# Attention results with features on the partitions (values stationary, two heads at once) and a feature-major second gate, in a two-block transformer kernel

## The chip, the core and the metric

The kernel runs on one core of a Trainium2 chip. A core has five engines, each with its own queue of instructions in fixed order: TensorE (PE; matmuls and transposes), VectorE (DVE), ScalarE (ACT), GpSimd (POOL) and SyncE (SP), which mostly issues transfers. Engines wait for each other on semaphores. The metric is the device time of one execution in microseconds (us); less is better.

## The reference

Two transformer blocks run one after the other on 256 tokens of width 1024, in float32.

```python
# first block, cut
fox_out  = softmax(q k^T/8 + forget bias, causal) @ v              # 8 heads of 64
diff_out = (softmax(q1 k1^T + alibi) - lam*softmax(q2 k2^T + alibi)) @ v   # 4 heads, v of 128
diff_out = _rms(diff_out, diff_norm_g[l]) * (1.0 - lam_init)
mixed = concatenate([fox_out, diff_out], axis=-1)
x = x + g1 * (mixed @ w_out[l])
h2 = _modulate(x, ln2_g[l], sh2, sc2)
x = x + g2 * ((silu(h2 @ w_gate[l]) * (h2 @ w_up[l])) @ w_down[l])
# second block, cut
za_u, za_v, q, k, v_att, g_a, g_b = split(rms_norm(x) @ w_in)
y_a = sgu_mixer(gelu(za_u), gelu(za_v), ...)
y_b = moba_attention(q, k, v_att, rel_bias)                        # 16 heads of 64
merged = sigmoid(g_a) * y_a + sigmoid(g_b) * y_b
x = x + merged @ w_out
x = x + square(relu(rms_norm(x) @ w_ff1)) @ w_ff2
x = x + sigmoid(rms_norm(x) @ w_ple_gate) * (p @ w_ple_proj)
return rms_norm(x)
```

## The kernel before

**Tiles.** The 256 tokens are two tiles t of 128 tokens on the partitions. A float32 matrix is split in a high and a low part: for a weight, ScalarE writes `wh` (a rounded copy of `raw`, which a transfer brought) and VectorE `wl` (raw minus wh). A product is then three matmuls, high by high, high by low and low by high (`mm3`); such three are called a triple here. A matmul of plain float32 operands (PV, the statistics `ap` and `pb`) is one instruction in the program and two records in the trace. Attention results and norm inputs are split in the same way (`mTh`, `mTl`).

**Attention.** `attention()` (L726 to L773) serves the fox attention (name `fa`) and the two halves of the moba attention (`ma0`, `ma1`), each of 8 heads. For a tile t and a pair of head groups it makes `scores` (s), `softmax` (VectorE adds the bias and takes the maximum, ScalarE exponentiates, which leaves unnormalised probabilities and their sums), four transposes (`tr4`, pt), a copy on ScalarE (pT), and PV: pT is the stationary operand (128 columns), the values of one head (64 columns) are moving, and the result (`pv`) has tokens on the partitions. When all groups of t are done, VectorE multiplies `pv` by the reciprocal sums into `mixed` or `yb`. Names read as attention, t, first head of the pair, member: fa120 is tile 1, pair 2, member 0. `diff_group` (L966 to L1023, name `da`) does this for the difference attention with its own normalisation (the two probabilities are scaled and subtracted before the transposes), its PV (`dpv`), and at the end a root mean square over each head: square (dsq) on ScalarE, sum (dss) on VectorE, an inverse root (dn) on GpSimd, multiplication into `mixed`, four transposes (mt) and the split into `mTh`, `mTl`. `fox_out` (L1035 to L1044) transposes the fox half of `mixed` (mf) and splits it.

**Out-projection.** `out_proj` (L1171 to L1185) takes the halves h of the features (0 fox, 1 diff), in each the tiles t, in each two column blocks of 512: four triples each, so 24 matmuls for a half and a tile. `wo` is the first block's, `wo2` the second's. Behind it come the residual (rg, x on VectorE), the second norm (n2j, n2x on ScalarE, n2a, n2r on GpSimd, transposes n2t) and `up`, the first product of the feed-forward part.

**Second block.** `ga` and `gb` are the two gates; `gate` (L1641) takes each in tiles of tokens (weights moving, 512 columns), and `merge` (L1658 to L1671) adds the two branches, transposes the sum (mt2) and splits it for `wo2`.

**What sets the order.** The instructions of all engines are written out by generators that a planner steps: it keeps a clock for each engine from its own table of costs and runs a generator on when what it waits for should be there. `slot` asks for room in the accumulators, `flag` for another generator's mark, `on` and `onp` for data. `room` (L723) opens a new attention group only while `groups[0]` is under a limit, which is 3 in this part; a fox pair adds 2 at its start and each member takes 1 off behind its PV; a diff group adds and takes 1. One piece of work is kept as filler for TensorE: the products `ppa` of the last stage (p @ w_ple_proj), given away in pieces where the planner sees TensorE idle, once the out-projection's mark is set (`spare`, L1295). What comes out is one fixed queue for each engine.

Of the kernel before, what the change touches and what calls it, by code (L numbers as in the profile page):

```python
# [10 lines left out]
F32 = mybir.dt.float32  # L11
# [6 lines left out]
P = 128  # L18
# [188 lines left out]
def body(ctx, tc, ins, out):  # L207
# [144 lines left out]
    def on(*aps, slack=None):  # L352
        return lambda: pace.when(*aps) <= clock["PE"] + (par(SLACK) if slack is None else slack)
# [275 lines left out]
    use(("dk", 1), True)  # L629


    def piece(acc, x_, k, u, first, last, a=0):

        for j in range(4):
            wh, wl = use(k, h=j // 2)
            kt = u * 4 + j
# [86 lines left out]
    def room():  # L723
        return groups[0] < par(ROOM)

    def attention(qT, kT, bias, extra, row, vt, vflag, dst, name):  # L726

        state = {}

        def pair(t, n, heads):  # L730
            yield slot(2), room, calm
            groups[0] += 2
            nm = f"{name}{t}{n}"
            for q, sp in enumerate(scores(qT, kT, heads, t, extra, nm)):
                run(group(t, sp, heads[q], f"{nm}{q}"))

        def group(t, sp, heads, nm):
            yield on(sp[:, :len(heads) * (t + 1) * P])
            pe, sm = yield from softmax(sp, heads, t, bias, None if row is None else row(t), nm)
            yield onp(pe), slot()  # L740
            rs = state[t]["rs"]
            V.reciprocal(rs.rearrange("p (a b) -> p b a", b=2)[:, heads[0] % 2, heads[0] // 2:heads[0] // 2 + len(heads)],
                         sm[:, :len(heads)])
# [24 lines left out]
        def launch():  # L768
            for t in range(NT):
                state[t] = {"rs": small(f"{name}{t}rs", 8), "n": len(HG[t])}  # L770
# [31 lines left out]
    mixed = [slab(f"mixed{t}") for t in range(NT)]  # L802

    def log_forget(z, e, lf):

# [141 lines left out]
    def fox_start():  # L947
        yield flag("fox_qk", "fox_c")
        attention(fqkT[0], fqkT[1], lambda h, nk: al[:, 4, 256 - nk:256], (selr, R), fox_row,
                             lambda k: vv[k][:, 0:512], "fv1", [m[:, 0:512] for m in mixed], "fa")  # L950


    def keep(dst, kflag, scale=None):
# [12 lines left out]
    def diff_group(t, n, h0, gs):  # L966
# [39 lines left out]
        if dstate[t]["n"]:  # L1006
# [8 lines left out]
        V.tensor_tensor(mixed[t][:, 512:1024].rearrange("p (h d) -> p h d", d=P), pv.rearrange("p (h d) -> p h d", d=P),  # L1015
                        r.unsqueeze(2).broadcast_to([P, 4, P]), op=ALU.mult)
        free(pv)
        yield onp(mixed[t][:, 512:1024]), slot(), lambda: len(mT) > t
        pt = tr4(mixed[t][:, 512:1024], 4, f"mt{t}")
        yield on(pt)  # L1020
        split_act(pt, 4, mT[t][0], mT[t][1], 4, pfs("dng"))
        free(pt)
        flags.add(f"mT1{t}")  # L1023

# [5 lines left out]
            for n, h0 in enumerate(range(0, 4, gs)):  # L1030
                run(diff_group(t, n, h0, gs))

    mT = []

    def fox_out():  # L1035
        for t in range(NT):
            yield flag("fa0", "fa1"), onp(mixed[t][:, 0:512]), slot()
            mT.append((slab(f"mTh{t}", F32R).rearrange("p (k t) -> p k t", t=P),
                       slab(f"mTl{t}", F32R).rearrange("p (k t) -> p k t", t=P)))
            pt = tr4(mixed[t][:, 0:512], 4, f"mf{t}")  # L1040
            yield on(pt)
            split_act(pt, 4, mT[t][0], mT[t][1], 0)
            free(pt)
            flags.add(f"mT0{t}")  # L1044

    rows2, bz, ap2 = {}, {}, {}
# [83 lines left out]
    run(lam(), 2)  # L1132
    run(diff_qk())
    run(diff())
    run(fox_out())
# [35 lines left out]
    def out_proj(name, mTs, mflag, fin):  # L1171
        acc = {}
        for h in range(2):
            for t in range(NT):
                until(flag(f"{mflag}{h}{t}"))
                until(on(mTs[t][0][:, h * 4:h * 4 + 4, :], mTs[t][1][:, h * 4:h * 4 + 4, :]))
                for cb in range(2):
                    if h == 0:
                        acc[t, cb] = psA(f"{name}{t}{cb}")
                    piece(acc[t, cb], mTs[t], (name, h, cb), h, h == 0, h == 1)  # L1180
# [117 lines left out]
    run(ple_prep())  # L1298
    run(ple_proj(), 2)
    hT_n, *hT_all = hT_tiles("n2")  # L1300
    out_proj("wo1", mT, "mT", residual(0, norm_shift("n2", hT_n, "n2")))
    hT = hT_n


    def feature_piece(acc, k, f):


        for kt in range(KT):
            wh, wl = use(k + (kt // 4,), h=kt % 4 // 2)
            c = slice((kt % 4) * 512 + f * P, (kt % 4) * 512 + f * P + P)  # L1310
            T.matmul(acc, lhsT=wh[:, c], rhs=hT_all[2][:, kt, :], start=kt == 0, stop=False)
            T.matmul(acc[:, 0:256], lhsT=wl[:, c], rhs=hT_all[0][:, kt, :], start=False, stop=kt == KT - 1)
            if kt % 2 and kt < KT - 1:
                tick()

# [215 lines left out]
            return self.d[self.k + (t,)] if self.k else self.d[t]  # L1531

    rs3 = Late(rstd, "n3")
    yb = [slab(f"yb{t}") for t in range(NT)]
    vm = [slab(f"vm{t}") for t in range(NT)]

    rrow = half("rrow")
# [36 lines left out]
    for hf in range(2):  # L1574
        qk = [slab(f"{nm}T{hf}").rearrange("p (a t) -> p a t", t=256) for nm in ("q", "k")]
        proj(("v", hf), keep(lambda t: vm[t][:, hf * 512:(hf + 1) * 512], f"mv{hf}", rs3), None if hf else "n3")
        proj_T(("q", hf), qk[0], 0, f"mq{hf}")
        proj_T(("k", hf), qk[1], 1, f"mk{hf}")

        def moba(hf=hf, qk=qk):  # L1580
            yield flag(*(f"m{c}{hf}{f}" for c in "qk" for f in range(4))), on(qk[0], qk[1])
            attention(qk[0], qk[1], lambda h, nk: rev(hbs[0][:, hf * 8 + h, 0:nk]), None, None,
                                 lambda k: vm[k][:, hf * 512:(hf + 1) * 512], f"mv{hf}1",
                                 [y[:, hf * 512:(hf + 1) * 512] for y in yb], f"ma{hf}")
        run(moba())


# [65 lines left out]

    for hf in range(2):
        proj(("ga", hf), gate(ya, hf, "ya"))
    mT2 = []

    def merge(t, hf):  # L1658
        yield flag(f"gya{hf}{t}")
        c = slice(hf * 512, hf * 512 + 512)  # L1660
        V.tensor_tensor(yb[t][:, c], yb[t][:, c], ya[t][:, c], op=ALU.add)
        if not mT2:
            for q in range(NT):
                mT2.append((slab(f"m2h{q}", F32R).rearrange("p (k t) -> p k t", t=P),
                            slab(f"m2l{q}", F32R).rearrange("p (k t) -> p k t", t=P)))
        yield onp(yb[t][:, c]), slot()
        pt = tr4(yb[t][:, c], 4, "mt2")
        yield on(pt)
        split_act(pt, 4, mT2[t][0], mT2[t][1], 4 * hf)
        free(pt)  # L1670
        flags.add(f"mU{hf}{t}")  # L1671

    for hf in range(2):
        proj(("gb", hf), gate(yb, hf, f"ma{hf}", merge))
    st["phase"] = 3
    until(lambda: len(mT2) == 2)
    out_proj("wo2", mT2, "mU", residual(None, norm_plain("n4", Lazy("n4"), pcs("nffn"), "n4", after4)))
    hT = lazy("n4")
    hT_all = late["n4"][1:]
    st["phase"] = 4  # L1680
# [220 lines left out]
```

## Time and profile before

| | |
|---|---|
| runs (us) | 786.88, 786.51, 786.5; median 786.51 |
| profiled execution | 787.08 us, its span 785.3 us |
| TensorE busy | 770.6 us (98%) |
| VectorE, ScalarE busy | 520.4 us (66%), 424.9 us (54%) |
| GpSimd busy | 34.4 us |
| the chain that ended last | PE 91%, ACT 3%, DVE 3%, issue 1%, DMA 1% |

The sum of an edit is made against the profiled execution, whose rows give the durations: 0.57 us above the median. All helpers record the line L153, so groups are told apart by the names of their tiles, written out<-in.

### The profile page before, as it was taken

To read this page: it belongs to the slowest core of one execution; us is meant where nothing else is said; L and a number is where in the kernel's file an instruction comes from. 1 tells how busy PE (TensorE), PEld (TensorE's weight loads), DVE (VectorE), ACT (ScalarE), POOL (GpSimd) and SP (SyncE) were. 2 spreads that over 40 slices of the span, in tenths; PEclk is the share of its full clock that TensorE was granted. 3 is DMA by queue.
4 is the path that set the end of the run, shared out by engine and by line. 5 is a ranking of instruction groups with operands and counts; after the bars stand their busy time and mean duration, and the time that the engine had idled before them with its cause. 6 is when DMAs were issued, how large, how long until landed. Compare 5 with 4: busy or idle time off the path is not lost.

```text
span 785.3 us, 10687 instructions
## 1 busy us (share of the span) xinstructions
PE 770.6 (98%) x4110; PEld 631.6 (80%) x4110; DVE 520.4 (66%) x913; ACT 424.9 (54%) x711; POOL 34.4 (4%) x73
## 2 busy tenths in 40 slices
PE   8999999999999999999999999999999999999996
PEld 7777667778888888888879878888888888888885
DVE  4878867667576866558674658746676665566583
ACT  4457467466554554456556584554475455445463
POOL 0000000121100000001100001000010000000011
PEclk9999999999999999999999999999999999999999
DMA  8967853755855666534762334545555544554331
GB/s 338 413 245 300 291 192 126 285 220 193 321 214 215 240 230 227 199 124 159 297 214 68 148 108 161 215 167 209 187 174 203 190 162 184 214 214 183 138 108 54
DMA packets 25251, 159.61 MB, mean 203 GB/s; under 512 B 2944, under 2 KB 3104, under 8 KB 8816
## 3 DMA queue, kind: packets, MB, share of 16 engines
q1 hardware_dynamic: 23184, 152.27, 52.0%
q0 software_dynamic: 2016, 6.66, 2.5%
q8 instruction: 32, 0.52, 0.3%
q14 instruction: 19, 0.16, 0.1%
HBM read 156.80 MB, written 2.12 MB: 202 GB/s over the span
## 4 chain that ended last, share of the span: by engine, by line
PE 91%; ACT 3%; DVE 3%; issue 1%; DMA 1%; POOL 0%; SPq 0%; POOLq 0%; ACTq 0%; DVEq 0%
PE up L153 27%; PE dn L153 19%; PE wo L153 5%; PE pa L153 3%; PE pga L153 3%; PE gb L153 3%; PE ga L153 3%; PE zu L153 3%; PE v L153 2%; PE zv L153 2%; PE dk L153 1%; PE k0T L153 1%; PE q0T L153 1%; PE q1T L153 1%; PE ap L153 1%; PE k1T L153 1%
## 5 line engine op out<-in xcount | busy, mean ns | idle before, releaser
L153 DVE TENSOR_TENSOR wl<-raw,wh 128x1024 fp32r<-128x1024 f32 (+3 forms) x218 | 278.7, 1309 | 109.0 <-ACT wh L153 108.9
L153 ACT ACTIVATE wh<-raw 128x1024 fp32r<-128x1024 f32 (+3 forms) x218 | 235.8, 1124 | 66.2 <-PE up L153 14.2
L153 PE MATMUL up<-n2b,wh 128*128 128x512 f32 x320 | 114.4, 401 | 0.0
L153 PE MATMUL up<-n2b,wl 128*128 128x256 f32 x320 | 89.8, 281 | 0.0
L153 PE MATMUL dn<-wh,aTh 128*128 128x512 f32 x216 | 84.9, 393 | 0.0
L153 PE MATMUL dn<-wl,aTh 128*128 128x512 f32 x216 | 84.3, 390 | 0.0
L153 PE MATMUL dn<-wh,aTl 128*128 128x512 f32 x216 | 84.1, 390 | 0.0
L153 PE MATMUL up<-n4b,wh 128*128 128x512 f32 x224 | 79.5, 399 | 0.0
L153 PEld LDWEIGHTS up<-n2b,wh 128*128 128x128 f32 x320 | 60.1, 188 | 15.6 <-issue 1.1
L153 ACT ACTIVATE fs<-up 128x256 f32<-128x256 f32 x68 | 25.9, 381 | 83.9 <-PE up L153 83.9
L153 PE MATMUL up<-n4b,wl 128*128 128x256 f32 x224 | 62.9, 281 | 0.0
L153 PEld LDWEIGHTS up<-n2b,wl 128*128 128x128 f32 x320 | 60.4, 189 | 1.0 <-issue 0.5
L153 DVE TENSOR_TENSOR fs<-up,fs 128x256 f32<-128x256 f32 x68 | 28.7, 422 | 39.7 <-ACT fs L153 39.5
L153 PEld LDWEIGHTS up<-n4b,wh 128*128 128x128 f32 x224 | 42.1, 188 | 10.3
L153 PEld LDWEIGHTS dn<-wl,aTh 128*128 128x128 f32 x216 | 40.6, 188 | 8.9
L153 PEld LDWEIGHTS dn<-wh,aTh 128*128 128x128 f32 x216 | 40.6, 188 | 8.5
L153 PEld LDWEIGHTS dn<-wh,aTl 128*128 128x128 f32 x216 | 40.6, 188 | 7.9
L153 PEld LDWEIGHTS up<-n4b,wl 128*128 128x128 f32 x224 | 42.3, 189 | 0.3
L153 ACT ACTIVATE aTh<-fs 128x512 fp32r<-128x512 f32 x24 | 15.2, 632 | 37.4 <-DVE fs L153 37.4
L153 DVE TENSOR_TENSOR aTl<-fs,aTh 128x512 fp32r<-128x512 f32 x24 | 16.6, 693 | 16.6 <-ACT aTh L153 16.5
L153 PE MATMUL pa<-wh,h1b 128*128 128x512 f32 x96 | 24.5, 400 | 0.8 <-ACT h1b L153 0.6
L153 PE MATMUL v<-wh,n3b 128*128 128x512 f32 x64 | 20.9, 405 | 0.6 <-DVE n3b L153 0.6
(686 smaller groups left out, 1393.5 us busy)
## 6 DMA issues: line engine op xcount, KB each, us to landing
raw<-in_ws_dram SPq DMA_DIRECT2D x112, 1024.0 KB, 4.8
raw<-in_ada_dram SPq DMA_DIRECT2D x16, 1024.0 KB, 5.0
raw<-in_ada_dram SPq DMA_DIRECT2D x16, 512.0 KB, 10.9
raw<-in_wko_dram SPq DMA_DIRECT2D x8, 768.0 KB, 9.6
bias<-rd POOLq DMA_DIRECT2D x1, 2048.0 KB, 10.7
x<-in_x_dram SPq DMA_DIRECT2D x2, 512.0 KB, 7.2
pp<-ppo POOLq DMA_DIRECT2D x2, 512.0 KB, 3.6
ppt<-pp POOLq DMA_DIRECT2D x2, 512.0 KB, 3.9
```

The lines of the kernel that those rows point to most:

```text
L153: r = f(*a, **k)
```

## The change

The probabilities of `attention` are normalised before the transposes (a reciprocal and one VectorE multiplication for each head of a group). PV of a pair then runs once both members have their pT: the values are stationary (64 columns), pT is moving (128 columns), and even and odd heads write partitions 0 to 63 and 64 to 127 of the same accumulator. Its result has features on the partitions. For fox it is split into `mTh`, `mTl` directly, and `fox_out` with its eight transposes is gone; for moba ScalarE copies it to `ybT`. `groups[0]` falls by 2 at once behind the PV of the pair. The `gb` gate has the weights stationary and all 256 tokens moving (`feature_piece3`), and `merge` works on pairs of feature blocks.

```diff
-        def group(t, sp, heads, nm):
+        def group(t, sp, heads, pair_, both, nm):
...
+            V.reciprocal(sm[:, :n], sm[:, :n])
+            for i in range(n):
+                c = slice(i * nk, (i + 1) * nk)
+                V.tensor_scalar(pe[:, c], pe[:, c], sm[:, i:i + 1], None, op0=ALU.mult)
             yield onp(pe), slot()
...
             pt = tr4(pe, 4, nm + "pt")
             yield on(pt)
-            pT = copy_T(pt, nm)
+            both[heads[0] % 2] = copy_T(pt, nm)
             free(pt)
-            yield onp(pT), flag(vflag)
+            if len(both) < 2:
+                return
+            yield onp(both[0], both[1]), flag(vflag)
...
-            for i, h in enumerate(heads):
+            for i, hs in enumerate(zip(*pair_)):
                 for k in range(t + 1):
                     b = i * (t + 1) + k
-                    T.matmul(pv[:, h * 64:(h + 1) * 64], lhsT=pT[:, b * P:(b + 1) * P],
-                             rhs=vt(k)[:, h * 64:(h + 1) * 64], start=k == 0, stop=k == t)
-            groups[0] -= 1
-            state[t]["n"] -= 1
+                    for q, h in enumerate(hs):
+                        T.matmul(pv[64 * q:64 * q + 64, (h // 2) * P:(h // 2 + 1) * P],
+                                 lhsT=vt(k)[:, h * 64:(h + 1) * 64], rhs=both[q][:, b * P:(b + 1) * P],
+                                 start=k == 0, stop=k == t)
+            groups[0] -= 2
+            state[t]["n"] -= 2
             if state[t]["n"] == 0:
                 yield on(pv)
-                V.tensor_tensor(dst[t].rearrange("p (h d) -> p h d", d=64), pv.rearrange("p (h d) -> p h d", d=64),
-                                rs.unsqueeze(2).broadcast_to([P, 8, 64]), op=ALU.mult)
+                take(t, pv)
...
+    def fox_take(t, pv):
+        split_act(pv, 4, *mixed_T(t), 0)
+        flags.add(f"mT0{t}")
...
+    def feature_piece3(acc, k, f):
+
+        for kt in range(KT):
+            wh, wl = use(k + (kt // 4,), h=kt % 4 // 2)
+            c = slice((kt % 4) * 512 + f * P, (kt % 4) * 512 + f * P + P)
+            T.matmul(acc, lhsT=wh[:, c], rhs=hT_all[0][:, kt, :], start=kt == 0, stop=False)
+            T.matmul(acc, lhsT=wh[:, c], rhs=hT_all[1][:, kt, :], start=False, stop=False)
+            T.matmul(acc, lhsT=wl[:, c], rhs=hT_all[0][:, kt, :], start=False, stop=kt == KT - 1)
...
+    def merge(hf, p, acc):
...
+        V.tensor_tensor(a3(sg), a3(acc), rrow[:, 256:512].unsqueeze(1).broadcast_to([P, 2, 256]), op=ALU.mult)
+        yield on(sg, slack=par(ESLACK))
+        S.activation(sg, sg, AF.Sigmoid)
+        yield flag(f"ma{hf}0", f"ma{hf}1"), on(sg, ybT[hf], slack=par(ESLACK))
+        V.tensor_tensor(a3(sg), a3(sg), ybT[hf][:, k, :], op=ALU.mult)
...
+                T.transpose(pt[:, j * 256 + t * P:j * 256 + (t + 1) * P], ya[t][:, f:f + P], ident)
...
+        V.tensor_tensor(sg, sg, pt, op=ALU.add)
...
+        S.activation(hi[:, k, :], a3(sg), AF.Copy)
+        yield on(hi[:, k, :], slack=par(ESLACK))
+        V.tensor_tensor(lo[:, k, :], a3(sg), hi[:, k, :].bitcast(F32), op=ALU.subtract)
```

The order of the queues moves with it. In the fences below `wh` and `wl` are the two parts of a weight, `pf` holds the identity matrix, and numbers tell buffers apart. TensorE before, at the transposes of the last diff group (da11pt), inside the out-projection:

```order
L153 MATMUL da11pt<-pf,da110p 128x128 x4
L153 MATMUL wo_1460<-wh_1079,mTh_1279 128x512
L153 MATMUL wo_1460<-wh_1079,mTl_1280 128x512
L153 MATMUL wo_1460<-wl_1080,mTh_1279 128x512
L153 MATMUL wo_1460<-wh_1079,mTh_1279 128x512
L153 MATMUL wo_1460<-wh_1079,mTl_1280 128x512
L153 MATMUL wo_1460<-wl_1080,mTh_1279 128x512
L153 MATMUL dpv_1406<-vv_589,da11pT 128x128
L153 MATMUL dpv_1406<-vv_590,da11pT 128x128
L153 MATMUL dpv_1406<-vv_589,da11pT 128x128
L153 MATMUL dpv_1406<-vv_590,da11pT 128x128
L153 MATMUL wo_1496<-wh_1028,mTh_1306 128x512
```

TensorE after, at the same transposes:

```order
L153 MATMUL wo_1325<-wl_1365,mTh_1140 128x512
L153 MATMUL da11pt<-pf,da110p 128x128 x4
L153 MATMUL dpv_1545<-vv_589,da11pT 128x128
L153 MATMUL dpv_1545<-vv_590,da11pT 128x128
L153 MATMUL dpv_1545<-vv_589,da11pT 128x128
L153 MATMUL dpv_1545<-vv_590,da11pT 128x128
L153 MATMUL mt_1597<-pf,mixed 128x128 x4
L153 MATMUL n2t_1607<-pf,n2x_1604 128x128 x4
L153 MATMUL n2t_1617<-pf,n2x_1604 128x128 x4
L153 MATMUL wo_1384<-wh_1252,mTh_1360 128x512
```

Before, these steps stand in the first half of `wo` with triples of it between them; now they stand behind the second half's tile 0 (wo_1325), directly behind one another, and tile 1 of that half (wo_1384) follows them.

VectorE before, where da110 and da111 are scaled for those transposes:

```order
L153 TENSOR_TENSOR sc_597<-sc_597,pc 128x4
L153 RECIPROCAL da110sm<-da110sm 128x2
L153 RECIPROCAL da111sm<-da111sm 128x2
L153 TENSOR_SCALAR da111sm<-da111sm,nlam 128x2
L153 TENSOR_SCALAR da111p<-da111p,da111sm 128x256
L153 SCALAR_TENSOR_TENSOR da110p<-da110p,da110sm,da111p 128x256
L153 TENSOR_SCALAR da111p<-da111p,da111sm 128x256
L153 SCALAR_TENSOR_TENSOR da110p<-da110p,da110sm,da111p 128x256
L153 TENSOR_TENSOR wl_1445<-raw_1346,wh_1444 128x2048
```

VectorE after, at the same scaling:

```order
L153 TENSOR_TENSOR rg<-wo_1297,bias_82 128x512
L153 TENSOR_TENSOR x_71<-x_71,rg 128x512
L153 TENSOR_TENSOR wl_1537<-raw_1436,wh_1536 128x2048
L153 RECIPROCAL da110sm<-da110sm 128x2
L153 RECIPROCAL da111sm<-da111sm 128x2
L153 TENSOR_SCALAR da111sm<-da111sm,nlam 128x2
L153 TENSOR_SCALAR da111p<-da111p,da111sm 128x256
L153 SCALAR_TENSOR_TENSOR da110p<-da110p,da110sm,da111p 128x256
L153 TENSOR_SCALAR da111p<-da111p,da111sm 128x256
L153 SCALAR_TENSOR_TENSOR da110p<-da110p,da110sm,da111p 128x256
```

Before, the scaling stood ahead of a weight subtraction of 2048 columns; now one stands ahead of it, with the residual's two steps.

## Rows read from the trace of the kernel before

**Rows 1.** The page's first part: engine, busy us (share), instructions.

```profile
PE 770.6 (98%) x4110; PEld 631.6 (80%) x4110; DVE 520.4 (66%) x913; ACT 424.9 (54%) x711; POOL 34.4 (4%) x73
```

**Rows 2.** TensorE's waits: us in total, times, longest us.

```profile
PE fa001pt L153 <- DVE fa100mx L153: 0.8, 1, 0.8
PE n2t L153 <- ACT n2x L153: 0.8, 2, 0.4
PE v L153 <- DVE n3b L153: 0.6, 1, 0.6
```

**Rows 3.** Stretches: us, then busy us and count of each engine.

```profile
139.30:166.60 27.30, 27.30 (x143) 21.52 (x143) 19.65 (x31) 12.02 (x14) 3.27 (x6) 1.00 0.71 277
166.60:174.00 7.40, 6.95 (x34) 5.10 (x32) 4.63 (x8) 5.26 (x14) 3.67 (x7) 1.00 0.55 211
```

**Rows 4.** Chain of waits, in time order: start us, us, what.

```profile
104.77 1.73 PE fa0pv L153 x16
...
142.16 0.44 PE mt L153 x4
...
145.81 0.89 PE dpv L153 x8
...
506.20 21.77 PE ga L153 x96
```

**Rows 5.** TensorE's timeline, statistics stage: start us, us, engine, line, operation.

```profile
99.37 1.02 PE L153 MATMUL pb<-bz,ones 128*128 128x512 f32 x2
100.33 1.06 PE L153 MATMUL ap<-raw,condz 128*32 128x512 f32 x8
101.32 0.74 PE L153 MATMUL fv<-wh,h1b 128*128 128x512 f32 x2
```

**Rows 6.** TensorE's timeline, last gate, at its change to 256 columns.

```profile
771.60 0.40 PE L153 MATMUL pga<-wh,n5b 128*128 128x256 f32 x2
771.84 0.28 PE L153 MATMUL pga<-wl,n5b 128*128 128x256 f32 x1
771.96 0.40 PE L153 MATMUL pga<-wh,n5b 128*128 128x256 f32 x2
```

**Rows 7.** Timeline of all engines, the chain behind da11's transposes.

```profile
144.46 0.60 ACT L153 ACTIVATE da11pT<-da11pt 128x512 f32<-128x512 f32 x1 [1.14 <-PE da11pt L153]
...
146.74 0.60 ACT L153 ACTIVATE dsq<-dpv 128x512 f32<-128x512 f32 x1 [1.68 <-PE dpv L153]
...
147.66 0.68 DVE L153 TENSOR_REDUCE dss<-dsq 128x4 f32<-128x512 f32 x1
...
148.71 1.03 POOL L153 TENSOR_TENSOR dn1y<-dn1a,mhalf 128x4 f32<-128x4 f32 x1
...
150.05 0.69 DVE L153 TENSOR_TENSOR mixed<-dpv,dn1y 128x512 f32<-128x512 f32 x1
...
154.03 0.69 ACT L153 ACTIVATE mTh<-mt,pf 128x512 fp32r<-128x512 f32 x1 [2.87 <-PE mt L153]
```

**Rows 8.** VectorE's timeline, maxima and scaling of diff groups.

```profile
130.44 0.41 DVE L153 CUSTOM_DVE_ANT_0 da110p<-da110s,bias 128x256 f32<-128x256 f32 x1
...
131.32 0.16 DVE L153 RECIPROCAL da100sm<-da100sm 128x2 f32<-128x2 f32 x1
...
131.83 0.35 DVE L153 TENSOR_SCALAR da101p<-da101p,da101sm 128x256 f32<-128x256 f32 x1
...
133.41 2.29 DVE L153 TENSOR_TENSOR wl<-raw,wh 128x2048 fp32r<-128x2048 f32 x1
```

**Rows 9.** ScalarE's timeline: exponential, weight copy, norm scaling.

```profile
138.22 0.50 ACT L153 ACTIVATE da111p<-da111p,da111mx 128x256 f32<-128x256 f32 x1
...
139.89 1.92 ACT L153 ACTIVATE wh<-raw 128x2048 fp32r<-128x2048 f32 x1 [0.59 <-DMA raw<-in_ws_dram]
...
168.88 1.34 ACT L153 ACTIVATE n2x<-x,n2r 128x512 f32<-128x512 f32 x2 [2.11 <-POOL n2r L153]
```

More of the change, by code (lines that the diff above doesn't have):

```diff
@@ L629, in body, with piece @@
     use(("dk", 1), True)
-    def piece(acc, x_, k, u, first, last, a=0):
+    def piece(acc, x_, k, u, first, last, a=0, k0=None):
         for j in range(4):
             wh, wl = use(k, h=j // 2)
-            kt = u * 4 + j
+            kt = (u * 4 if k0 is None else k0) + j
             c = slice(j * 512 + a, j * 512 + a + acc.shape[-1])
@@ L724, in room, with attention @@
         return groups[0] < par(ROOM)
-    def attention(qT, kT, bias, extra, row, vt, vflag, dst, name):
+    def attention(qT, kT, bias, extra, row, vt, vflag, take, name):
         state = {}
@@ L733, in pair @@
             nm = f"{name}{t}{n}"
+            both = {}
             for q, sp in enumerate(scores(qT, kT, heads, t, extra, nm)):
-                run(group(t, sp, heads[q], f"{nm}{q}"))
-        def group(t, sp, heads, nm):
-            yield on(sp[:, :len(heads) * (t + 1) * P])
-            pe, sm = yield from softmax(sp, heads, t, bias, None if row is None else row(t), nm)
+                run(group(t, sp, heads[q], heads, both, f"{nm}{q}"))
+        def group(t, sp, heads, pair_, both, nm):
+            n = len(heads)
+            nk = (t + 1) * P
+            yield on(sp[:, :n * nk])
+            pe, sm = yield from softmax(sp, heads, t, bias, None if row is None else row(t), nm)
+            yield on(pe, sm[:, :n], slack=par(ESLACK))
+            V.reciprocal(sm[:, :n], sm[:, :n])
+            for i in range(n):
+                c = slice(i * nk, (i + 1) * nk)
+                V.tensor_scalar(pe[:, c], pe[:, c], sm[:, i:i + 1], None, op0=ALU.mult)
             yield onp(pe), slot()
-            rs = state[t]["rs"]
-            V.reciprocal(rs.rearrange("p (a b) -> p b a", b=2)[:, heads[0] % 2, heads[0] // 2:heads[0] // 2 + len(heads)],
-                         sm[:, :len(heads)])
             pt = tr4(pe, 4, nm + "pt")
             yield on(pt)
-            pT = copy_T(pt, nm)
+            both[heads[0] % 2] = copy_T(pt, nm)
             free(pt)
-            yield onp(pT), flag(vflag)
+            if len(both) < 2:
+                return
+            yield onp(both[0], both[1]), flag(vflag)
             if "pv" not in state[t]:
@@ L769, in launch @@
             for t in range(NT):
-                state[t] = {"rs": small(f"{name}{t}rs", 8), "n": len(HG[t])}
+                state[t] = {"n": len(HG[t])}
                 for n in range(0, len(HG[t]), 2):
@@ L801, in body @@
     vv = [slab(f"vv{t}") for t in range(NT)]
-    mixed = [slab(f"mixed{t}") for t in range(NT)]
+    mixed = slab("mixed")
+    mixed = [mixed[:, t * 512:(t + 1) * 512] for t in range(NT)]
     def log_forget(z, e, lf):
@@ L949, in fox_start @@
         attention(fqkT[0], fqkT[1], lambda h, nk: al[:, 4, 256 - nk:256], (selr, R), fox_row,
-                             lambda k: vv[k][:, 0:512], "fv1", [m[:, 0:512] for m in mixed], "fa")
+                             lambda k: vv[k][:, 0:512], "fv1", fox_take, "fa")
     def keep(dst, kflag, scale=None):
@@ L1014, in diff_group @@
         V.tensor_scalar(r, r, 1.0 - LAM_INIT, None, op0=ALU.mult)
-        V.tensor_tensor(mixed[t][:, 512:1024].rearrange("p (h d) -> p h d", d=P), pv.rearrange("p (h d) -> p h d", d=P),
+        V.tensor_tensor(mixed[t].rearrange("p (h d) -> p h d", d=P), pv.rearrange("p (h d) -> p h d", d=P),
                         r.unsqueeze(2).broadcast_to([P, 4, P]), op=ALU.mult)
         free(pv)
-        yield onp(mixed[t][:, 512:1024]), slot(), lambda: len(mT) > t
-        pt = tr4(mixed[t][:, 512:1024], 4, f"mt{t}")
+        yield onp(mixed[t]), slot()
+        pt = tr4(mixed[t], 4, f"mt{t}")
         yield on(pt)
-        split_act(pt, 4, mT[t][0], mT[t][1], 4, pfs("dng"))
+        split_act(pt, 4, *mixed_T(t), 4, pfs("dng"))
         free(pt)
@@ L1031, in diff, with mixed_T @@
                 run(diff_group(t, n, h0, gs))
[L1033 to L1044, printed above, removed]
+    mT = {}
+    def mixed_T(t):
+        if t not in mT:
+            mT[t] = tuple(slab(f"mT{q}{t}", F32R).rearrange("p (k t) -> p k t", t=P) for q in "hl")
+        return mT[t]
+    def fox_take(t, pv):
+        split_act(pv, 4, *mixed_T(t), 0)
+        flags.add(f"mT0{t}")
     rows2, bz, ap2 = {}, {}, {}
@@ L1134, in body @@
     run(diff())
-    run(fox_out())
     proj(("dk",), dk_heads)
@@ L1175, in out_proj @@
                 until(flag(f"{mflag}{h}{t}"))
-                until(on(mTs[t][0][:, h * 4:h * 4 + 4, :], mTs[t][1][:, h * 4:h * 4 + 4, :]))
+                m = mTs(h, t)
+                until(on(*m))
                 for cb in range(2):
@@ L1179, in out_proj @@
                         acc[t, cb] = psA(f"{name}{t}{cb}")
-                    piece(acc[t, cb], mTs[t], (name, h, cb), h, h == 0, h == 1)
+                    piece(acc[t, cb], m, (name, h, cb), h, h == 0, h == 1, k0=0)
                     if t == NT - 1:
@@ L1300, in body @@
     hT_n, *hT_all = hT_tiles("n2")
-    out_proj("wo1", mT, "mT", residual(0, norm_shift("n2", hT_n, "n2")))
+    out_proj("wo1", lambda h, t: [q[:, 4 * h:4 * h + 4, :] for q in mT[t]], "mT", residual(0, norm_shift("n2", hT_n, "n2")))
     hT = hT_n
@@ L1312, in feature_piece @@
             T.matmul(acc[:, 0:256], lhsT=wl[:, c], rhs=hT_all[0][:, kt, :], start=False, stop=kt == KT - 1)
+            if kt % 2 and kt < KT - 1:
+                tick()
+    def feature_piece3(acc, k, f):
[5 more added lines that the diff above has]
+            T.matmul(acc, lhsT=wl[:, c], rhs=hT_all[0][:, kt, :], start=False, stop=kt == KT - 1)
             if kt % 2 and kt < KT - 1:
@@ L1533, in body @@
     rs3 = Late(rstd, "n3")
-    yb = [slab(f"yb{t}") for t in range(NT)]
+    ybT = [slab(f"ybT{hf}").rearrange("p (a t) -> p a t", t=256) for hf in range(2)]
     vm = [slab(f"vm{t}") for t in range(NT)]
@@ L1583, in moba @@
                                  lambda k: vm[k][:, hf * 512:(hf + 1) * 512], f"mv{hf}1",
-                                 [y[:, hf * 512:(hf + 1) * 512] for y in yb], f"ma{hf}")
+                                 lambda t, pv: S.activation(ybT[hf][:, :, t * P:(t + 1) * P],
+                                                            pv.rearrange("p (a t) -> p a t", t=P), AF.Copy), f"ma{hf}")
         run(moba())
@@ L1655, in body @@
         proj(("ga", hf), gate(ya, hf, "ya"))
[L1656 to L1667, printed above, removed]
+    mT2 = [[], []]
@@ new lines, in merge @@
+    def merge(hf, p, acc):
+        k = slice(2 * p, 2 * p + 2)
+        a3 = lambda ap: ap.rearrange("p (k t) -> p k t", t=256)
+        yield on(acc), flag("rrow")
+        sg = half("sgm")
+        V.tensor_tensor(a3(sg), a3(acc), rrow[:, 256:512].unsqueeze(1).broadcast_to([P, 2, 256]), op=ALU.mult)
[3 more added lines that the diff above has]
+        V.tensor_tensor(a3(sg), a3(sg), ybT[hf][:, k, :], op=ALU.mult)
+        yield flag(f"gya{hf}0", f"gya{hf}1"), onp(ya[0], ya[1]), slot()
+        pt = psB(f"mt2{hf}{p}")
+        for j in range(2):
+            for t in range(NT):
+                f = (4 * hf + 2 * p + j) * P
+                T.transpose(pt[:, j * 256 + t * P:j * 256 + (t + 1) * P], ya[t][:, f:f + P], ident)
@@ L1668, in merge @@
         yield on(pt)
-        split_act(pt, 4, mT2[t][0], mT2[t][1], 4 * hf)
+        V.tensor_tensor(sg, sg, pt, op=ALU.add)
         free(pt)
-        flags.add(f"mU{hf}{t}")
-    for hf in range(2):
-        proj(("gb", hf), gate(yb, hf, f"ma{hf}", merge))
+        if not mT2[hf]:
+            mT2[hf] = [slab(f"m2{q}{hf}", F32R).rearrange("p (k t) -> p k t", t=256) for q in "hl"]
+        hi, lo = mT2[hf]
+        yield on(sg, slack=par(ESLACK))
+        S.activation(hi[:, k, :], a3(sg), AF.Copy)
@@ new lines, in merge @@
+        yield on(hi[:, k, :], slack=par(ESLACK))
+        V.tensor_tensor(lo[:, k, :], a3(sg), hi[:, k, :].bitcast(F32), op=ALU.subtract)
+        flags.add(f"mu{hf}{p}")
+        if f"mu{hf}{1 - p}" in flags:
+            flags.update(f"mU{hf}{t}" for t in range(NT))
+    for hf in range(2):
+        for p in range(2):
+            acc = psA(f"gb{hf}{p}")
+            for f in range(2):
+                feature_piece3(acc[:, f * 256:(f + 1) * 256], ("gb", hf), 2 * p + f)
+            if p:
+                for u in range(2):
+                    done(("gb", hf, u))
+            run(merge(hf, p, acc), 0)
+            tick()
@@ L1675, in body @@
     st["phase"] = 3
-    until(lambda: len(mT2) == 2)
-    out_proj("wo2", mT2, "mU", residual(None, norm_plain("n4", Lazy("n4"), pcs("nffn"), "n4", after4)))
+    until(lambda: mT2[0])
+    out_proj("wo2", lambda h, t: [q[:, :, t * P:(t + 1) * P] for q in mT2[h]], "mU", residual(None, norm_plain("n4", Lazy("n4"), pcs("nffn"), "n4", after4)))
     hT = lazy("n4")
```

## The prediction

> **What bounds the kernel now.** I read the page's table of engines first: TensorE is busy 770.6 of 785.3 us, VectorE 520.4 [rows 1]. So the time is TensorE's instruction stream plus its holes, 14.7 us in all. Second, TensorE's waits: inside the program none is longer than 0.8 us; the ones that the change touches are the transposes of a fox group behind VectorE (0.8 once), those of the second norm behind ScalarE (0.8 in two), and the third norm's first use (0.6) [rows 2]. Third, busy time by stretch: from 139.3 to 166.6 us, the out-projection `wo`, TensorE is busy 27.30 of 27.30 us, and in the 7.4 us behind it (`ppa` and the second norm) 6.95 [rows 3]. An edit can thus help by what it takes out of TensorE's stream, and can hurt by any hole that it opens. The work that feeds TensorE runs on engines with room in total, but each has a queue in fixed order, and so has TensorE. The profile gives the durations; the order of the changed program tells where a queue puts each step.
>
> **PV with the values stationary.** Before, 8 matmuls of 64 moving columns against loads of 128 columns make a block of 16 records, 1.73 us [rows 4]. There are 9 such blocks (three attentions; one for the first query tile, two for the second). After, a block is again 8 matmuls, but of 128 moving columns into partitions 0–63 or 64–127, alternating. One matmul of 128 f32 columns is two records at 0.111 us each (dpv: 8 in 0.89) [rows 4]. Whether the two column halves run at once is not shown for halves, but it is for quarters: two f32 records of 512 columns over the whole array take 0.96 us, and the eight of `ap`, in four column tiles, 0.99 [rows 5]; one after the other they would be 3.84. If halves do the same, a block is 8 x 0.111 = 0.89, plus the switch into and out of the tiles: from 0.99 against 8/4 x 0.43 (0.86, a record at the 0.111 per 128 columns being 0.44), 0.14, to perhaps 0.4 where narrow streams hide loads less. I take 1.2 us, so 9 x -0.53 = **-4.8 us**; lower end 1.03 (-6.3). If halves don't overlap, 16 x 0.111 + 0.35 = 2.1, +0.4 a block, +3.5: the upper end. I lie at the lower side since `ap` is the same kind of instruction.
>
> Here a rule speaks against the change. `ap` uses all 128 rows for its column tiles and still runs four wide [rows 5]. The Trainium skill, TensorE: Matmul & The Clock Gate, Part 3 (The mechanism), says that a weight load overlaps matmuls in flight only when its row group differs; the two halves of a pair have the same rows, so by it their loads would not be hidden. The trace of `ap` disagrees as far as 512 columns can tell, and no row shows 128. By that rule the sum would be the upper end, +3.5 in place of -4.8.
>
> **The fox transposes go.** Two blocks of 4 (0.44 us each, as mt) [rows 4]: **-0.9**. Their copies on ScalarE and VectorE stay, reading the PV result instead. Nothing waits longer: the out-projection's first half now depends on each tile's own PV, and it starts earlier.
>
> **Scaling before the transposes.** 18 groups gain a reciprocal and two 128x256 or four 128x128 multiplications on VectorE (0.35 for a 256-wide one) [rows 8], about 1 us each, 18 us on an engine that is idle a third of the time [rows 1]. In the moba halves it lies before the transposes, and the PV of two groups waits for the second one's copy. For the first moba half TensorE has projections queued there, so nothing. In the second there is little left to queue: three times a copy of 0.6 us (as da11pT) [rows 7] ends after TensorE arrives: **+2.0** (0 to 3.5).
>
> **The second gate feature-major.** 96 matmuls of 512 columns (21.77 us for `ga`, the same kind) [rows 4] become 192 of 256. `pga` shows those: a triple every 0.36 us, 0.120 each [rows 6], so 23.04: **+1.3**. The merge becomes finer: its last low part on VectorE stands behind a weight subtraction, and the third triple of `wo2`'s second half needs it: **+0.8** (0 to 2.3, one subtraction as in rows 8). The fourth `ppa` accumulation (12 matmuls) is moved to the third norm and covers its wait: **-0.5** [rows 2].
>
> **The out-projection's order.** This is the large term. A pair of fox groups now gives back its places in `groups` only after both PVs, so `room` opens later for the diff groups, and the queues change. Before, da11's scores stood in `dv`, far ahead, and its transposes, PV and `mt` had triples of `wo` between each (the first fence of the change's section); every step of that chain was covered [rows 3]. After, the scores of da110 and da111 come only when the whole first half of `wo` is done, and da11pt, dpv, mt and the norm's transposes stand in one piece with no `wo` between; the 24 matmuls of `wo` for the second tile and all of `up` are queued behind. I follow it from the end of those scores, T0.
>
> TensorE: `ap` twice (2.0) [rows 5], eight triples of `wo` (0.68 each by `ga`, 5.4), pb (8 records, 0.9), da10pt 0.44, dpv 0.89 [rows 4]: it reaches da11pt at T0+9.6. VectorE and ScalarE: da10pt is over on TensorE at about T0+6.0; its copy (0.6 and a handover) ends at 6.8, then two exponentials of da111 (0.5 each), 7.8, then the copy `wh` of 1.92 [rows 9], 9.7. On VectorE `wl` (2.29) stands ahead of da110's scaling in its queue (the second fence), so it ends at 12.0; the scaling is 2.1 (131.32 to 133.41) [rows 8], 14.1; the last transposes 14.3. TensorE idles 14.3 - 0.4 - 9.6 = 4.2 us. Before, that subtraction stood behind the scaling.
>
> From there the chain runs bare: copy 0.6, dpv 0.89, square 0.6, from the reduction to the end of `mixed` 3.1 (147.66 to 150.74, GpSimd's 1.03 within), three handovers 0.4; mt 0.44, `mTh` 0.69 [rows 4, 7], the norm's scaling n2x 1.34 behind it on ScalarE [rows 9], its last four transposes 0.44, handovers 0.4. That is 8.9 us, in which TensorE works 2.2 (dpv, mt, eight transposes): 6.7 idle. With small waits at the start of the stage (a statistics sum behind its copy, a low part behind its high part; 0 to 1.5, I take 0.8) the stage gains 4.2 + 6.7 + 0.8 = **+11.7**. It is not cancelled by `ppa`: those 48 matmuls still run, but behind it. What goes are the waits of the fox group and of the second norm's transposes, **-1.6** [rows 2].
>
> **Sum.** -4.8 - 0.9 + 2.0 + 1.3 + 0.8 - 0.5 + 11.7 - 1.6 = +8.0. The profiled run took 787.08, 0.57 over the median of the three runs; 787.08 + 8.0 - 0.57 = **794.5 us**.
>
> **Rivals.**
> (1) Not slower: the hole stays small. The savings without the stalls are 4.8 + 0.9 + 0.5 + 1.6 - 1.3 = 6.5 us; if all new idle time is under that, the kernel wins. The place is da11pt: were da110's scaling done when TensorE arrives (the subtraction ahead of it not waiting for `wh`), 4.2 goes; with the moba copies and the low part of `wo2` covered and PV at 1.03 us a block it is -6.3 - 0.9 - 0.5 - 1.6 + 1.3 + 6.7 = -1.3, 785.2. For it: VectorE has a third of its time free. Against: the fixed order on three engines, and 6.7 that remain.
> (2) Only the hole ahead of da11pt vanishes, the rest as forecast: +8.0 - 4.2, 790.3. It decides with the end of `wh` for da11's neighbour: 4 us earlier would do.
> (3) The column halves don't overlap: +3.5 in place of -4.8, 802.8. Against it the quarters [rows 5]; for it that no row shows halves with streams so short.
> (4) The change doesn't do what it says, that is, PV's saving is there but lies under waits for copies: TensorE idle by as much in each block: +4.8, 799.3. Against it: only the second moba half lacks queued work.
>
> **How the numbers follow.** Forecast 794.5 (its own range 791 to 799): 0.55. Rival 2: 0.14. Rival 1: 0.15. Rival 3: 0.09. Rival 4: 0.07. The range 787.5 to 802 holds the forecast, rivals 2 and 4 and a little of 1 and 3, about 0.8. A measurement can tell 0.2%, 1.6 us, from no change. Rival 1's 785.2 lies at that line: I give its lower part 0.09 as faster and 0.07 as within 0.2% (with a little of rival 2's lower end); the other cases are slower, 0.84.
>
> **What would show it.** TensorE's idle time between the transposes of da11 and the second half of `wo` for tile 1: 10 to 11 us right, under 5 wrong. VectorE's scaling of da110 right behind a 2048-wide subtraction. The waits for da11pt (on VectorE), mt (VectorE), n2t (ScalarE) at the top of TensorE's list. A block of fa1pv in 1.0 to 1.4 us; 2 or more means no overlap. The gate `gb` in 23 us with no idle time in it. Most wrong I would be if the chain's steps started earlier than the order allows me to see, or if a transfer that I took as landed were late, since the weights of `wo` are asked for at other places now.

## The result, and the profile after

The changed kernel takes 816.82 us (median of four runs, 816.65 to 818.95), the kernel before 786.5 beside it: a ratio of 1.0391, 95% interval 1.0373 to 1.0409. It is slower, as forecast, but by 30.3 us and not by 8, and outside the range. The profiled execution has a span of 814.9 us, 29.6 over that of before.

The first part of the page of the changed kernel, and then TensorE's list of waits (us in total, times, longest), answer to [rows 1] and [rows 2]:

```profile
PE 778.0 (95%) x4198; PEld 632.8 (78%) x4198; DVE 532.4 (65%) x958; ACT 428.5 (53%) x714; POOL 32.9 (4%) x73
```

```profile
PE up L153 <- DVE wl L153: 9.6, 8, 2.0
PE da11pt L153 <- DVE da110p L153: 3.8, 2, 3.4
PE mt L153 <- DVE mixed L153: 3.8, 1, 3.8
PE dn L153 <- ACT wh L153: 1.5, 1, 1.5
PE n2t L153 <- ACT n2x L153: 1.4, 1, 1.4
```

TensorE is busy 7.4 us longer, though it has less to do, and idle 36.9 us in place of 14.7. Two places stand in the list. The waits for da11pt, mt and n2t are those that the prediction named, in its order. The longest group it didn't name at all: `up`, in the first feed-forward part, waits for the low part of its weights, eight times.

First the named one. The timeline of all engines, from the end of the first column blocks of `wo` to its second tile (start us, us, engine, operation, in brackets the idle time before it and what ended that); it answers to [rows 7 to 9]:

```profile
153.15 1.90 ACT L153 ACTIVATE wh<-raw 128x2048 fp32r<-128x2048 f32 x1
...
155.08 2.29 DVE L153 TENSOR_TENSOR wl<-raw,wh 128x2048 fp32r<-128x2048 f32 x1 [1.92 <-ACT wh L153]
...
158.74 0.44 PE L153 MATMUL da11pt<-pf,da110p 128*128 128x128 f32 x2 [3.44 <-DVE da110p L153]
...
160.90 2.07 PE L153 MATMUL dpv<-vv,da11pT 128*128 128x128 f32 x8 [0.69 <-ACT da11pT L153]
...
166.75 1.11 PE L153 MATMUL mt<-pf,mixed 128*128 128x128 f32 x4 [3.79 <-DVE mixed L153]
...
169.26 1.97 PE L153 MATMUL n2t<-pf,n2x 128*128 128x128 f32 x8 [1.39 <-ACT n2x L153]
...
170.88 0.78 PE L153 MATMUL wo<-wh,mTh 128*128 128x512 f32 x1
```

`wh`, then `wl`, then the scaling, and only then the transposes: the order read off the queues held step by step. TensorE idles 9.7 us here. But dpv takes 2.07 us where TensorE's timeline of the kernel before has 1.05, and mt 1.11 where it has 0.60:

```profile
145.65 1.05 PE L153 MATMUL dpv<-vv,da11pT 128*128 128x128 f32 x8
...
153.40 0.60 PE L153 MATMUL mt<-pf,mixed 128*128 128x128 f32 x4
```

The same stretch of the changed kernel in steps of 2 us shows why (us, TensorE busy and its records, granted clock, the transfers' share, GB/s):

```profile
156.00:158.00 2.00, 0.00 (x0) 1.00 0.00 0
158.00:160.00 2.00, 0.91 (x4) 0.88 0.73 229
160.00:162.00 2.00, 1.31 (x6) 0.50 0.71 295
...
170.00:172.00 2.00, 2.00 (x9) 0.50 0.00 0
172.00:174.00 2.00, 2.00 (x8) 0.70 0.00 0
174.00:176.00 2.00, 2.00 (x11) 1.00 0.04 8
```

Behind the first idle time the granted clock is 0.50, the lower of its two levels (1.2 GHz), and stays there until 173 us; up to 169 us TensorE works in short pieces with waits between them, and from then on without a gap. That costs 0.3 (the second half of da11pt, 0.69 against 0.44 for the first), 1.0 (dpv), 0.5 (mt), 0.5 (n2t, 1.62 to the next start against 1.10 before) and 1.2 us (the first six matmuls of `wo`, 2.53 in place of 1.36): 3.5 us in all.

Now the other place, the first feed-forward part. Whole stretches (columns as before, with the other engines between; the first row is of after, the second of before; the row of after leaves out some 60 matmuls of `up`, which stand ahead of 200 us beside `ppa`):

```profile
200.00:393.00 193.00, 180.64 (x900) 149.05 (x899) 115.42 (x146) 88.52 (x132) 4.69 (x9) 0.97 0.52 191
```

```profile
174.00:364.00 190.00, 189.67 (x980) 159.46 (x981) 125.83 (x164) 101.84 (x156) 6.83 (x13) 1.00 0.57 208
```

12.4 us idle against 0.3, and a mean clock of 0.97, which is some 6 us more by estimate (3% of 193). One of the waits, in rows of all engines of the changed kernel's timeline (SPq issues the transfers):

```profile
244.38 2.94 ACT L153 ACTIVATE wh<-raw 128x1024 fp32r<-128x1024 f32 x3
...
246.60 3.11 DVE L153 SCALAR_TENSOR_TENSOR bz<-raw,cond,bz 128x512 f32<-128x512 f32 x4
246.71 3.35 SPq L153 DMA_DIRECT2D raw<-in_ws_dram  x2
...
249.62 2.35 DVE L153 TENSOR_TENSOR wl<-raw,wh 128x1024 fp32r<-128x1024 f32 x2
250.89 0.38 PE L153 MATMUL up<-n2b,wl 128*128 128x256 f32 x1 [1.91 <-DVE wl L153]
...
251.54 1.06 ACT L153 ACTIVATE wh<-raw 128x1024 fp32r<-128x1024 f32 x1 [4.22 <-DMA raw<-in_ws_dram]
```

TensorE waits 1.91 us for a low part that VectorE begins at 249.62, some 0.6 us after the last product before it has ended. Its high part was there by 247.3 (the first row), but in VectorE's queue four steps that prepare a statistics product (bz, 3.11 us) stand ahead of the low part. The three other long waits (271.56, 292.99 and 312.38 us) have the same four steps ahead of them. ScalarE meanwhile waits 4.22 us for the next weight to land: the supply runs without a reserve, so a few us on VectorE show at once. Why there is none is told by the records of `ppa` (first and last start, of the changed kernel and then of the one before):

```profile
L153 PE MATMUL ppa<-wh,pTh x8: 389/389/499, 182.9 to 403.1; 128*128 128x512 f32 x8
```

```profile
L153 PE MATMUL ppa<-wh,pTh x8: 389/389/499, 166.3 to 172.9; 128*128 128x512 f32 x8
```

All four `ppa` accumulations use one weight, split in one of the kernel's four pairs of buffers (`NSP` in the code), and the pair comes free only behind the fourth. Each accumulation is two triples, six matmuls. Two stand ahead of `up` and the third inside it (191.6 us); the planner found no idle time for the fourth there, and gave it away behind the third norm, inside `v` (402.4 us). Until 403 us three pairs serve the feed-forward part in place of four.

### The profile page after: what moved, and what is told of

It is laid out like the page before. It is cut to its first block, busy times and chain, and to the rows that moved or that the text cites. A ratio compares the mean times of both kernels' runs of the same rounds, so it can differ in the third digit from the quotient of the medians.

```text
span 814.9 us, 10913 instructions
## 1 busy us (share of the span) xinstructions
PE 778.0 (95%) x4198; PEld 632.8 (78%) x4198; DVE 532.4 (65%) x958; ACT 428.5 (53%) x714; POOL 32.9 (4%) x73
## 4 chain that ended last, share of the span: by engine, by line
PE 80%; DVE 8%; ACT 6%; issue 5%; DMA 1%; POOL 1%; SPq 0%; POOLq 0%; DVEq 0%; ACTq 0%
PE up L153 24%; PE dn L153 15%; DVE wl L153 4%; PE pa L153 3%; PE gb L153 3%; PE v L153 3%; PE pga L153 3%; PE ga L153 3%; PE zu L153 3%; ACT wh L153 3%; PE wo L153 3%; PE zv L153 2%; PE ap L153 2%; PE dk L153 1%; PE fv L153 1%
## 5 line engine op out<-in xcount | busy, mean ns | idle before, releaser
L153 PE MATMUL up<-n2b,wh 128*128 128x512 f32 x320 | 118.6, 411 | 0.2 <-ACT wh L153 0.2
L153 PE MATMUL up<-n2b,wl 128*128 128x256 f32 x320 | 92.1, 288 | 9.7 <-DVE wl L153 9.6
L153 PEld LDWEIGHTS up<-n2b,wh 128*128 128x128 f32 x320 | 61.9, 193 | 16.7 <-ACT wh L153 1.1
L153 PEld LDWEIGHTS up<-n2b,wl 128*128 128x128 f32 x320 | 62.1, 194 | 14.1 <-DVE wl L153 12.6
L153 PEld LDWEIGHTS up<-n4b,wh 128*128 128x128 f32 x224 | 42.1, 188 | 10.3
L153 PE MATMUL gb<-n3b,wh 128*128 128x256 f32 x128 | 23.4, 285 | 0.0
```

Source lines behind the costliest of these rows:

```text
L153: r = f(*a, **k)
```

## The experiments

**Held buffer or lost lead.** Two theories could explain the waits of `up`. One is the held buffer. The other is a lost lead: no weight transfer is issued from 157.4 to 179.0 us, since nothing moves in the hole, and the feed-forward part might never catch up. The first one heals with `ppa`, the second with the hole. Three edits of the changed kernel, and one of the kernel before, ran on one chip beside the kernel before (786.72 us there; the changed kernel's 816.82 is from the earlier measurement, with 786.5 beside it). In the cuts, `pps` is a list that grows by one with each `ppa` accumulation:

```diff
# a_ppa: the fourth ppa follows the third
-        return st["idle"] and "wo1" in flags
+        return "wo1" in flags and (st["idle"] or len(pps) == 3)
# a_early: each member of a pair gives its place back behind its own pT
             free(pt)
+            groups[0] -= 1
             if len(both) < 2:
...
-            groups[0] -= 2
# a_early_ppa: both
# b_ppheld: the kernel before, the fourth ppa held until the third norm
-        return st["idle"] and "wo1" in flags
+        return st["idle"] and "wo1" in flags and (len(pps) < 3 or st["phase"] == 2)
```

> The changed kernel, but the fourth ppa accumulation is given away right behind the third one, so that its weight's split buffer comes free before the feed-forward part. Theory (held buffer: with ppa's weight kept from 146 to 404 us the feed-forward part has three split buffers in place of four): the waits of up for wl (9.6 us) and the clock drops behind them go, the hole at da11pt stays: about 801 us, 799 to 803. Rival (lost lead: no weight was asked for from 157 to 179 us, and the feed-forward part never catches up): the waits of up stay, 814 to 817.

Measured: 799.01 us (two runs, 1.0 apart), 17.8 under the changed kernel. The waits of `up` for `wl` are gone from the list, the hole is still there, and the same part has 196.09 of 198 us busy at full clock:

```profile
178.00:376.00 198.00, 196.09 (x1008) 164.72 (x1007) 128.56 (x166) 103.87 (x161) 8.50 (x17) 1.00 0.57 208
```

> The changed kernel, but each member of a fox pair gives back its place in groups behind its own pT, so that room opens as early as before; ppa stays as in the changed kernel. The order then has da11pt inside the first half of wo again. Theory (held buffer): the hole (9.7 us of waits, some 4 us of lower clock) goes, the waits of up for wl stay at 8 to 10 us: 801 to 804. Rival (lost lead): both go, 783 to 788.

Measured: 807.16 us (two runs, 2.1 apart), 9.7 under the changed kernel. The hole is gone, the waits of `up` are the same to a tenth:

```profile
PE up L153 <- DVE wl L153: 9.6, 8, 2.0
PE pt L153 <- DVE xn L153: 1.6, 1, 1.6
PE dn L153 <- ACT wh L153: 1.5, 1, 1.5
PE wo L153 <- DVE mTl L153: 1.2, 1, 1.2
PE ap L153 <- DVE da101mx L153: 1.1, 1, 1.1
```

So the lost lead falls. It came out 3 us above the range of the expectation; new small waits in this stage (the last two rows, at 160 and 130 us) are 2.3 us of that.

> The kernel before, with the fourth ppa accumulation held back until the third norm, as the changed kernel has it; nothing else. Theory (held buffer): up waits for wl some 8 to 12 us in the first feed-forward part, the clock drops behind the waits: 798 to 804. Rival (lost lead): no hole ahead of it, so nothing: 786 to 788.

Measured: 806.5 us against 786.72 for the kernel before: 19.8 us for the place of six matmuls, with nothing else changed in the program (the planner writes the queues anew). `up` waits for `wl` 10.2 us in nine, and the part's clock is 0.98:

```profile
PE up L153 <- DVE wl L153: 10.2, 9, 2.3
```

```profile
172.00:383.00 211.00, 196.53 (x978) 160.81 (x979) 127.30 (x163) 103.28 (x158) 6.98 (x14) 0.98 0.52 188
```

The held weight is shown from both sides: put into the kernel before it costs 19.8 us, taken out of the changed one it gives 17.8. That it works through the pool of four pairs is read in the code, where a weight is split only while a pair is free; no run had a fifth pair.

> Both edits in the changed kernel. Both theories: no hole and no waits of up for wl. What is left is PV (nine blocks at 1.02 in place of 1.73: -6.4), the fox transposes (-0.9), the second gate (+1.3) and small waits (0 to +4): 781 to 785, a little faster than before.

Measured: 789.42 us against 786.72, ratio 1.0033 (1.0021 to 1.0044). The two repairs add up (17.8 + 9.7 = 27.5, together 27.4), more closely than runs of one kernel that differ by 1 to 2 us can show. But it isn't the gain that both theories promised: TensorE is busy 767.8 us, 2.8 less than before, and the kernel is still 2.7 slower. What is left?

**Which half keeps the rest.** The second block alone, on the first block of before; and the first block alone with both repairs, on the second block of before:

```diff
# b_moba: the kernel before, with the changed attention and second gate for moba; fox as before
-    def attention(qT, kT, bias, extra, row, vt, vflag, dst, name):
+    def attention_tok(qT, kT, bias, extra, row, vt, vflag, dst, name):   # called for fox
...
+    def attention(qT, kT, bias, extra, row, vt, vflag, take, name):      # called for moba
# c_fox: a_early_ppa, with the changed attention for fox alone; moba and the second gate as before
-    def attention(qT, kT, bias, extra, row, vt, vflag, take, name):
+    def attention_f(qT, kT, bias, extra, row, vt, vflag, take, name):    # called for fox
...
+    def attention(qT, kT, bias, extra, row, vt, vflag, dst, name):       # called for moba
```

> Only the second block's half of the change: moba's PV with the values stationary and the feature-major second gate; the first block is that of the kernel before, so its queues and ppa are as before. Theory (the two losses lie in the first block alone): second block's queries to the end took 400.05 us before and 400.38 with both repairs, so 786.5 to 787.3, no change. Rival (moba's scaling and the gate cost some us by themselves that the first block's losses hide): 789 or more.

Measured: 787.19 us against 787.0, ratio 1.0003 (0.9994 to 1.0012): no change. By the chains of waits of the two kernels, the block gains 2.3 us from the same piece of `v` (27 records) to `ga` (105.98 us to 103.72) and loses 2.6 from there to the fourth norm's last transposes (72.21 to 74.83): PV's gain in the moba halves pays for the second gate and the waits there, and no more.

> Only the first block's half of the change (fox PV with the values stationary, no fox transposes), with both repairs: places given back early, ppa finished behind its third accumulation; the second block is that of the kernel before. TensorE's stream is 3.0 us shorter (three blocks by 0.71, transposes 0.9). Theory (the small waits of the run with both repairs, 1.1 for a statistics transfer's buffer, 1.2 for a low part, 1.2 around ppa, 0.8 before up's transposes, come with fox's scaling on VectorE): 788 to 789.5. Rival (they come from elsewhere and the shorter stream counts): 783 to 785.

Measured: 788.9 us, ratio 1.0023 (1.0014 to 1.0032). That is 1.9 us over the kernel before, and most of the rest of 2.7: it lies in fox. Its own waits are those of the run with both repairs:

```profile
PE wo L153 <- DVE mTl L153: 1.2, 1, 1.2
PE ap L153 <- DVE da101mx L153: 1.1, 1, 1.1
...
PE at L153 <- DVE sg L153: 0.7, 1, 0.7
PE up L153 <- ACT n2b L153: 0.6, 1, 0.6
...
PE ppa L153 <- ACT full L153: 0.6, 1, 0.6
```

Another way to let the groups in earlier is a limit of 4 in place of 3 in the first phase's parameters, with the places given back in pairs as in the changed kernel. It ran on c_fox (all lines below) and on a_ppa (the limit alone):

```diff
-PARAMS = ((0.2, 0.8, 2.5, 3, 3, 0.6, 1.5, 1, 0.1, 0.3),
+PARAMS = ((0.2, 0.8, 2.5, 4, 3, 0.6, 1.5, 1, 0.1, 0.3),
...
-            groups[0] -= 1
...
+            groups[0] -= 2
```

> As the run before, but with the limit of groups at 4 in place of giving places back early: the diff groups are then let in at other points of the queue. If the small waits depend on where the planner puts things, it moves by 1 to 4 us against the run before, to either side (784 to 790); if they come with the scaling itself, it stays within 0.8 us of it.

> The whole change with ppa finished behind its third accumulation and the limit of groups at 4: another order that lets the diff groups in early. Held-buffer theory: no waits of up for wl, no hole of 4 us: 784 to 791.

Measured: 795.34 us with fox alone, 795.53 with the whole change, both 6 us worse than giving places back early, and both above the range that was written down. In both, TensorE waits 4.1 us ahead of mt again. The place at which the planner lets the diff groups in is worth several microseconds; a higher limit alone doesn't give the old places back.

**The scaling.** Fox's 16 multiplications stand on VectorE ahead of the diff groups' work. Left out, or put on another engine:

```diff
-                V.tensor_scalar(pe[:, c], pe[:, c], sm[:, i:i + 1], None, op0=ALU.mult)
+                pass                                                                     # c_fox_nosc
+                S.activation(pe[:, c], pe[:, c], AF.Copy, scale=sm[:, i:i + 1])          # c_fox_act
+                G.tensor_scalar(pe[:, c], pe[:, c], sm[:, i:i + 1], None, op0=ALU.mult)  # c_fox_pool
```

> The run with only the first block's half and both repairs (788.9), with the multiplication of the fox probabilities by the reciprocal sums left out, so the fox results stay unnormalised; the reciprocals stay. Theory (the 3 us of TensorE work that fox saves are given back because VectorE's twenty scaling steps push the diff chain back in its queue): the diff groups are let in about as early as in the kernel before and it is 783 to 785. Rival (the waits come from the pairing, a PV that waits for two copies, or from wo's earlier start): 787.5 to 789.5.

Measured: 784.58 us against 786.78, ratio 0.9971 (0.9961 to 0.9982); 4.3 under the run that scales (4.1, each taken against the kernel before beside it). The second diff `mt` stands at 147.89 us in place of 156.15 (TensorE's timelines of the run without scaling and of c_fox), and none of the small waits listed above is left:

```profile
147.89 0.60 PE L153 MATMUL mt<-pf,mixed 128*128 128x128 f32 x4
```

```profile
156.15 0.60 PE L153 MATMUL mt<-pf,mixed 128*128 128x128 f32 x4
```

So the scaling, not the pairing, gives back what fox's PV saves. The timelines show where it enters: with it the transposes of fa000 start 10.3 us behind the start of its last scores, without it 6.7; those of da00 17.3 and 9.7. How much of the 4 us is VectorE's time and how much the other order that the planner then writes isn't separated: each run has an order of its own.

> As the run with only the first block's half and both repairs, with fox's scaling on ScalarE (a copy with a scale) in place of VectorE. If the scaling's place on VectorE alone is the cost: 784 to 786.5. If the chain of scores, exponentials, scaling, transposes gets longer by it (a ScalarE copy of 128x256 takes some 0.5 us against 0.35) and the planner lets the diff groups in later, with mt standing without cover again: 790 to 797.

> The same with fox's scaling on GpSimd, which is busy 33 of 785 us. Its price there is shown by no row; bounds from its other rows, 0.2 to 1.7 us each. At 0.5 or less: 785 to 790; over 1 us, TensorE waits for the fox transposes by some us more: 792 to 800.

Measured: 802.89 and 802.69 us, 14 worse than on VectorE. So VectorE as the place of the scaling isn't the whole cost. On ScalarE the planner's order changes widely (the scores of fa100 stand at 109.2 us in place of 95.2), and TensorE waits twice each for a low part and for mt, 3.6 and 3.2 us at the longest:

```profile
PE wo L153 <- DVE mTl L153: 3.8, 2, 3.6
PE mt L153 <- DVE mixed L153: 3.6, 2, 3.2
PE wo L153 <- ACT mTh L153: 1.5, 2, 0.8
PE fa121pt L153 <- DVE mTl L153: 1.4, 1, 1.4
```

On GpSimd the transposes of a fox group wait for it (3.2 us in three), and mt again 2.8. Both fall in the upper of the two cases that were written down, and both lie above its range. No full version that beats the kernel before was found.

## Why the prediction was wrong

**The step that failed** is the sentence "The fourth `ppa` accumulation (12 matmuls) is moved to the third norm and covers its wait: -0.5". It costed the matmuls that moved (six of them, not 12: the trace of before has 24 matmuls of `ppa` in four accumulations, where the prediction speaks of 48), and its gain is there: the third norm's wait of 0.6 us [rows 2] is gone from the list. What it left out, a term put at nothing, is that the move lengthens the life of that weight's buffer by 230 us, so that `up` waits for low parts. The price is +17.8 (taken out) to +19.8 us (put in), some three fifths of the loss of 30.3 us. No rival held it either. The prediction followed queues, and this is a pool of buffers (four pairs), in which one pair held is a quarter of the supply.

**Right, and nearly to size: the hole.** Predicted 4.2 us idle ahead of da11pt and 6.7 in the chain behind it; measured 3.8 and 5.9 (0.7, 3.8, 1.4). The prediction's rival 2 (that the wait ahead of da11pt vanishes) is out: `wl` stood ahead of the scaling and the rows above show it waiting for `wh`. The size was short by the clock: 3.5 us at the lower level, which no term held. So the hole cost 13.2 us idle and slow, against 10.9 predicted (11.7 with the small waits at the start of the stage).

**PV: rival 3 is out.** Two steps of the changed kernel's chain of waits (start us, us), and the timeline of one pair (a row for each half), answer to [rows 4] and [rows 5]:

```profile
116.18 1.02 PE fa1pv L153 x16
```

```profile
555.10 7.19 PE gb L153 x60
```

```profile
116.11 0.32 PE L153 MATMUL fa1pv<-fa100pT,vv 128*64 128x128 f32 x1
116.11 0.32 PE L153 MATMUL fa1pv<-fa101pT,vv 128*64 128x128 f32 x1
```

The halves start together, and a block is 1.02 us, the lower end of the bounds, where I took 1.2: by that block nine save 6.4 in place of 4.8. The prediction weighed a rule of the Trainium skill, TensorE: Matmul & The Clock Gate, Part 3 (The mechanism): a weight load overlaps matmuls in flight only when its row group differs. The trace doesn't agree for halves with all 128 rows and 128 columns either: 16 records with as many loads in 1.02 us.

**The second gate** runs 60 matmuls in 7.19 us, 0.120 each as read from [rows 6]: 23.0 against 21.8 us, right.

**The moba halves and `wo2`**: predicted +2.0 and +0.8 of waits; the list of after has 0.8 for a PV behind its second copy and 0.5 for a low part. With -4.3 for PV and +1.3 for the gate that would be 1.7 us faster; the run with the second block alone is 0.2 slower (0.5 faster to 0.9 slower), so some 2 us of what the block loses stand in no row here.

**Scaling before the transposes** was costed only where TensorE would wait for it. For fox that was the wrong question: with it the chains of the fox and the diff groups come later. That is 4.3 us, by the run without it, and it was in no term.

**Rival 1** (not slower, with new idle time under 6.5 us) is out: idle time grew by 22.2 us. Nor would a small hole have been enough: with both losses repaired the kernel takes 789.4 us, 2.7 more than before, where the rival had 785.2. Only fox alone without its scaling, which isn't the change any more, comes under the kernel before (784.6).

## What to carry to other kernels

When an edit moves filler work, ask what the filler holds while it waits: a weight in a pool of four is a quarter of the supply for as long as its last use is put off, and the bill comes in a stage that the edit doesn't touch. When it adds a step to a chain, on an engine with time to spare too, look at which chains come later by it, and not only at the engine's share. And a hole in TensorE's stream is to be costed with the clock behind it: here 9.7 us of idle time brought 3.5 us of slow work.

## What the runs showed of the hardware

The granted clock fell to its lower level also behind waits as short as 1.9 us: in three of the four long waits of `up` (0.50 to 0.54 in the 2 us at 252, 272 and 314), and not in one (292.99 us, where it stayed at 1.00). Around the first of them, of the changed kernel, and last the one where it stayed:

```profile
250.00:252.00 2.00, 1.00 (x4) 0.92 0.88 307
252.00:254.00 2.00, 1.97 (x6) 0.50 1.01 418
254.00:256.00 2.00, 2.00 (x10) 0.72 1.03 434
```

```profile
256.00:260.00 4.00, 4.00 (x25) 1.00 0.81 291
```

```profile
292.00:294.00 2.00, 0.97 (x4) 1.00 0.89 295
```

In the first it came back some 3 us later, with TensorE busy throughout. A pair of 512 and 256 columns took 0.64 us in it against 0.35 (starts 252.41, 253.05, 253.69, then 256.08, 256.43), so each such drop costs about 1.5 us on top of the wait, by estimate (half of 3 us).
